# Triangular inverse of a decoder trunk: the eight transfers of inverted blocks into T issued from GpSimd, those into TT from SyncE

## The chip, the cores and the metric

The kernel runs on one core of a Trainium2 chip. A core has five engines with queues of their own: TensorE (PE in the profile, its weight loads PEld), VectorE (DVE), ScalarE (ACT), GpSimd (POOL) and SyncE (SP). An engine works through its queue in order; between engines only semaphores order the work. DMA transfers are issued from an engine's queue (here from SyncE, GpSimd and, a few, ScalarE) and run on the core's 16 DMA engines. The metric is device time in microseconds (us) of one execution.

## The reference, cut to what matters

A decoder trunk of two layers over 256 positions of width 1024. Each layer is a half-step gated feed-forward block, a mixer of two branches, and a second feed-forward block. The change lies in the mixer's gated delta-rule branch, which works in chunks of 64 positions for 8 heads:

```python
M = jnp.where(strict, jnp.einsum("bnhid,bnhjd->bnhij", kb, k) * decay, 0.0)
eye = jnp.eye(C, dtype=f32)
rhs = jnp.concatenate([v * beta[..., None], kb * jnp.exp(G)[..., None]], axis=-1)
sol = lax.linalg.triangular_solve(eye + M, rhs, left_side=True, lower=True, unit_diagonal=True)
```

The kernel does not solve; it inverts the unit lower triangular matrices `eye + M` (32 of 64 x 64, one for each head and chunk) and multiplies with the inverses.

## The kernel before, in words

**The stream of weights.** Nearly all of TensorE's work is products with weights that come once from HBM. SyncE loads them in blocks of 128 x 1024 (`wraw`, 512 KB, `load`, line 188) into five buffers in turn. ScalarE splits each block into a high part (`whi`, `prep`, through `act`, line 82), VectorE takes the rest (`wlo`, line 85), and TensorE multiplies with both (through `put`, line 60). A block's buffer comes free when VectorE is done with it, so SyncE's next load usually waits for VectorE.

**The order of the mixer.** The table `ORDER` (line 46) sets by hand in which order the pieces of the mixer are written: `k`, `q`, `v`, `z`, `b` and so on are products with weights, cut into steps; a capital `I` runs the generator `invert` on to its next `yield`. TensorE keeps that written order; the other engines' queues are set by a scheduler.

**The inverse** (`invert`, lines 925 to 986). The 32 matrices lie in pairs as 16 matrices of 128 x 128 in `Q`, each with 8 diagonal blocks of 16 x 16. The steps are:

1. Eight transfers bring the diagonal blocks of `Q` to DRAM (`dq1`), one transfer brings them back so that each partition holds one block (`X`).
2. VectorE inverts all 128 blocks at once in 15 steps (lines 941 to 945, tile `X2`) and writes the transposed copy beside them (line 946). The profile calls both `X`.
3. One transfer writes `X2` to DRAM (`dq2`, line 947; the profile says `dq`).
4. Sixteen transfers bring the inverted blocks back, one for each position on the diagonal: eight into `T` (line 950) and eight transposed into `TT` (line 951). Each moves 16 partitions x 16 matrices x 16 numbers, in runs of 64 bytes. `T` and `TT` were set to zero long before by GpSimd (line 789).
5. The blocks are joined to inverses of 32 and then of 64 (loop from line 961, `n` = 4 and 2): TensorE forms `yb` from `Q` and the odd column blocks of `TT`, ScalarE copies it out (`Y`), TensorE forms `wb` from `T` and `Y`, ScalarE copies that negated into `TT`, and for `n` = 4 VectorE turns 32 x 32 blocks of `TT` into `T` (line 985).

Between these products TensorE works at steps of `b3` (products `bc` in the profile), as `ORDER` has it: `b3:11 I b3:2 I b3:2 I b3`.

**Semaphores of transfers.** The scheduler gives SyncE's transfers eight completion semaphores in rotation, so a transfer waits until the eighth one ahead of it has landed. GpSimd's transfers have eight of their own. The first multiply of `yb` waits for four of the `TT` transfers (blocks 2, 4, 6 and 8); the first two multiplies of `wb` wait for four `T` transfers each, since one reads the left 64 columns of `T` and the other the right 64.

**GpSimd** does little: small powers for norms (line 227, `rsqrt`), products with them (line 889), zeroing (line 789), and transfers that add to their destination: weight blocks onto weight blocks (`wsum`, line 171) and partial sums onto `h` (line 494).

Of the kernel before, what the change touches and what calls it, by code (L numbers as in the profile page):

```python
# [51 lines left out]
def trunk_kernel(ctx, tc, x, wst, wsm, norms, lpar, rpar, cst, out):  # L52
    nc = tc.nc
    V, A, G = nc.vector, nc.scalar, nc.gpsimd
# [26 lines left out]
    def act(o, i, func=AF.Copy, **kw):  # L81
        return A.activation(out=o, in_=i, func=func, **kw)  # L82

    def tt(o, a, b, op):
        return V.tensor_tensor(out=o, in0=a, in1=b, op=op)  # L85
# [12 lines left out]
    def tmp2(name):  # L98
        return s2.tile([P, 512], F32, tag="s2", name=name)

    def trb(name):
        return trp.tile([P, 512], F32, tag="tr", name=name)
# [4 lines left out]
    def small(shape, name, bufs=2):  # L107
        return sm.tile(shape, F32, tag=name, name=name, bufs=bufs)
# [540 lines left out]
    def mixer(l, nxt):  # L649
# [135 lines left out]
        T = slots.tile([P, 16, P], F32, tag="sE", name="T")  # L785
# [139 lines left out]
        def invert():  # L925

            dq1 = dram.tile([P, 16, 16], F32, tag="dq1", name="dq1")
            dq2 = dram.tile([P, 2, 16, 16], F32, tag="dq2", name="dq2")
            for b in range(8):
                r0 = 16 * b  # L930
                nc.sync.dma_start(dq1[r0 : r0 + 16].rearrange("pr r s -> r pr s"), Q[r0 : r0 + 16, :, r0 : r0 + 16])
            X = s2.tile([P, 16, 16], F32, tag="s2", name="X")
            X2 = s2.tile([P, 2, 16, 16], F32, tag="s2", name="X2")
            with tc.issue_after(qev["ins"].ins):
                V.memset(X2[:], 0.0)
                V.memset(X2[:].rearrange("p a r s -> p (a r s)")[:, 0:256:17], 1.0)
            nc.sync.dma_start(X[:], dq1[:])
            yield
            Tl = X2[:, 0]
            tp = small([P, 64], "tp", 1)  # L940
            for c in range(15):
                n, m = 15 - c, c + 1
                t_ = tp[:, : n * m].rearrange("p (a b) -> p a b", a=n)
                tt(t_, X[:, c + 1 :, c : c + 1].to_broadcast([P, n, m]), Tl[:, c : c + 1, 0:m].to_broadcast([P, n, m]), ALU.mult)
                tt(Tl[:, c + 1 :, 0:m], Tl[:, c + 1 :, 0:m], t_, ALU.subtract)
            V.tensor_copy(X2[:, 1].rearrange("p r s -> p s r"), X2[:, 0])
            nc.sync.dma_start(dq2[:], X2[:])
            for b in range(8):
                r0 = 16 * b
                nc.sync.dma_start(T[r0 : r0 + 16, :, r0 : r0 + 16], dq2[r0 : r0 + 16, 0].rearrange("pr r s -> r pr s"))  # L950
                nc.sync.dma_start(TT[r0 : r0 + 16, :, r0 : r0 + 16], dq2[r0 : r0 + 16, 1].rearrange("pr r s -> r pr s"))
            yield

            def half_mm(bank, i, lhsT, rhs, w=64):
                for r in (0, 64):
                    PE.matmul(bank[r : r + 64, i * w : (i + 1) * w], lhsT[:, r : r + 64], rhs, start=True, stop=True)

            def odd(ap, n):
                return ap.rearrange("p (b o s) -> p b o s", b=n, o=2)[:, :, 1, :]

            for n in (4, 2):
                w = 64 // n
                order = (0, 1) if n == 4 else (1, 0)
                ys = [trb("yb") for _ in range(2)]
                ev = Y if n == 4 else [tmp2("Y2") for _ in range(2)]
                for half in order:
                    for i in range(8):
                        half_mm(ys[half], i, Q[:, 8 * half + i, :], odd(TT[:, 8 * half + i, :], n))
                    act(ev[half][:], ys[half][:])
                yield  # L970
                ws = [trb("wb") for _ in range(2)]
                for half in order:
                    for i in range(8):
                        half_mm(ws[half], i, T[:, 8 * half + i, :], ev[half][:, i * 64 : (i + 1) * 64])
                    pr = slice(8 * half, 8 * half + 8)
                    for b in range(n):
                        r0 = 2 * w * b
                        act(
                            TT[r0 : r0 + w, pr, r0 + w : r0 + 2 * w],
                            ws[half][r0 : r0 + w].rearrange("p (x b s) -> p x b s", x=8, b=n)[:, :, b, :],  # L980
                            scale=-1.0,
                        )
                        if n == 4 and b % 2 == 0:
                            blk = (slice(r0, r0 + 32), pr, slice(r0, r0 + 32))
                            V.transpose(out=T[blk], in_=TT[blk])
                yield
# [251 lines left out]
        def dn_branch(j):  # L1238
            yield from branch("d", 4, j)
            if j == 3:  # L1240
                m = tg[1]
                for t in range(2):
                    for n in range(2):
                        sl = slice(n * 512, (n + 1) * 512)
                        stt(m[:, t, sl], m[:, t, sl], 1.0, sums["d"][t][n][:], ALU.add, ALU.mult)

        sc, inv, rc = scalars(), invert(), recur()
        units = {"z": z_unit, "k": k_unit, "q": q_unit, "v": v_unit, "b": bcm, "d": zdm, "x": xs_unit, "g": gate, "N": dn_branch, "B": ss_branch}
        rests = {"K": k_rest, "Q": q_rest, "V": v_rest}
# [233 lines left out]
```

## Time and profile before

| | |
|---|---|
| time, median of 3 runs | 1536.88 us |
| lowest and highest | 1535.88 and 1537.06 us |
| the profiled execution's own time | 1536.77 us |
| its span, first to last instruction | 1534.5 us |
| busy share PE, DVE, ACT, POOL | 99%, 83%, 63%, 5% |
| granted TensorE clock | 0.999 |
| read from HBM | 291.43 MB, 191 GB/s over the span |
| share of the 16 DMA engines: q1 (SyncE), q0 (GpSimd) | 56.1%, 4.7% |

How to read it: the profile is one execution. A row of a timeline gives the start in us from the span's start, the duration, the engine, the line of the kernel, the operation, what it writes `<-` what it reads, and how many were merged (x). A bracket holds the idle time of the engine just before and what ended it. A letter q behind an engine's name (SPq, POOLq) means its queue, where transfers are issued: the duration of such a row is the issue, and the transfer itself ends later, at its landing. Lines of the helpers (60 for TensorE, 82 for ScalarE, 85 and 88 for VectorE) stand for many operations, so tiles tell them apart.

### The profile page before, as it was taken

The numbers are of one execution on the slowest core, as the hardware profiler recorded it, in microseconds if no ns is written. First come the engines' busy times: TensorE is split into PE (matmuls) and PEld (weight loads), VectorE is DVE, ScalarE is ACT, GpSimd is POOL, SyncE is SP. The second block draws the span as 40 slices with busy tenths as digits, with TensorE's granted clock in tenths as the row PEclk, the third lists the DMA queues.
The fourth block names the chain that finished last, engine by engine and source line by source line (L and its number), as shares of the span: only waits on it lengthen the run. The fifth ranks groups of instructions, "written<-read, shape, count | busy, mean of one in ns | idle before, by whom it ended". The sixth has DMA issues, their size and how long they took to land.

```text
span 1534.5 us, 29046 instructions
## 1 busy us (share of the span) xinstructions
PE 1515.0 (99%) x11460; PEld 1382.4 (90%) x11460; DVE 1270.7 (83%) x1939; ACT 962.2 (63%) x1560; POOL 79.8 (5%) x86
## 2 busy tenths in 40 slices
PE   8999999999999999999999999999999999999998
PEld 7999889989988888999999998899899888899997
DVE  6888978857999766888988889789579996688888
ACT  6656756865766645566665666587657765456655
POOL 0000010100000000000000002010000000000000
PEclk9999999999999999999999999999999999999999
DMA  7577666453656556667767767654455555556764
GB/s 286 183 227 237 194 214 209 143 151 126 206 167 204 166 178 208 190 197 241 222 207 223 227 196 229 207 183 138 154 183 160 189 188 169 182 173 205 232 219 138
DMA packets 95950, 297.33 MB, mean 194 GB/s; under 512 B 22517, under 2 KB 23493, under 8 KB 94790
## 3 DMA queue, kind: packets, MB, share of 16 engines
q1 hardware_dynamic: 91492, 282.56, 56.1%
q0 software_dynamic: 4032, 12.58, 4.7%
q8 instruction: 90, 1.47, 0.4%
q14 instruction: 46, 0.38, 0.1%
q10 hardware_dynamic: 290, 0.33, 0.1%
HBM read 291.43 MB, written 1.92 MB: 191 GB/s over the span
## 4 chain that ended last, share of the span: by engine, by line
PE 87%; DVE 6%; DMA 2%; ACT 2%; issue 2%; SPq 1%; POOL 0%; POOLq 0%; DVEq 0%; ACTq 0%
PE fc L60 29%; PE o L60 9%; PE t L60 9%; PE b L60 8%; PE p L60 7%; PE xs L60 4%; PE f L60 3%; PE kk L60 3%; PE bc L60 2%; PE zd L60 2%; PE qq L60 2%; DVE wlo L85 2%; DVE ca L88 2%; DMA wraw<-in_wst_dram 1%; PE ydb L60 1%
## 5 line engine op out<-in xcount | busy, mean ns | idle before, releaser
L85 DVE TENSOR_TENSOR wlo<-wraw,whi 128x1024 fp32r<-128x1024 f32 x464 | 559.7, 1221 | 110.1 <-ACT whi L82 105.0
L82 ACT ACTIVATE whi<-wraw 128x1024 fp32r<-128x1024 f32 x464 | 487.9, 1060 | 194.4 <-PE fc L60 43.8
L60 PE MATMUL fc<-uW,whi 128*128 128x256 f32 (+1 forms) x2600 | 444.1, 276 | 0.0
L60 PEld LDWEIGHTS fc<-uW,whi 128*128 128x128 f32 x2600 | 394.1, 188 | 3.1
L60 PE MATMUL fc<-uW,wlo 128*128 128x256 f32 x1280 | 356.2, 278 | 0.0
L60 PEld LDWEIGHTS fc<-uW,wlo 128*128 128x128 f32 x1280 | 240.6, 188 | 0.0
L60 PE MATMUL t<-whi,uW 128*128 128x512 f32 x512 | 168.0, 401 | 0.0
L82 ACT ACTIVATE whi<-wsum 128x1024 fp32r<-128x1024 f32 x80 | 85.0, 1063 | 79.0 <-PE fc L60 64.5
L85 DVE TENSOR_TENSOR wlo<-wsum,whi 128x1024 fp32r<-128x1024 f32 x80 | 97.6, 1224 | 30.9 <-ACT whi L82 27.9
L60 PEld LDWEIGHTS t<-whi,uW 128*128 128x128 f32 x512 | 95.5, 188 | 21.8 <-issue 2.4
L60 PE MATMUL t<-wlo,uW 128*128 128x512 f32 x256 | 100.4, 394 | 0.0
L60 PE MATMUL xs<-uW,whi 128*128 128x256 f32 x514 | 90.9, 280 | 0.0
L60 PEld LDWEIGHTS xs<-uW,whi 128*128 128x128 f32 x514 | 78.0, 188 | 0.3
L60 PE MATMUL b<-whi,bh 128*128 128x512 f32 x192 | 76.0, 396 | 0.0
L60 PE MATMUL b<-whi,bl 128*128 128x512 f32 x192 | 75.1, 391 | 0.0
L60 PE MATMUL b<-wlo,bh 128*128 128x512 f32 x192 | 74.8, 390 | 0.0
L60 PE MATMUL xs<-uW,wlo 128*128 128x256 f32 x256 | 71.0, 277 | 0.0
L60 PEld LDWEIGHTS t<-wlo,uW 128*128 128x128 f32 x256 | 48.1, 188 | 10.9 <-issue 1.0
L82 ACT ACTIVATE gh<-g 128x512 fp32r<-128x512 f32 x40 | 25.4, 634 | 44.1 <-DVE g L85 44.1
L82 ACT ACTIVATE whi<-wb 128x1024 fp32r<-128x1024 f32 x20 | 21.2, 1061 | 48.2 <-PE fc L60 45.3
L60 PE MATMUL p<-whi,bsa 128*128 128x512 f32 x144 | 49.0, 390 | 0.0
L60 PEld LDWEIGHTS xs<-uW,wlo 128*128 128x128 f32 x256 | 48.1, 188 | 0.0
(290 smaller groups left out, 3033.7 us busy)
## 6 DMA issues: line engine op xcount, KB each, us to landing
wraw<-in_wst_dram SPq DMA_DIRECT2D x464, 512.0 KB, 5.0
wsum<-in_wst_dram SPq DMA_DIRECT2D x20, 512.0 KB, 7.6
wb<-in_wst_dram SPq DMA_DIRECT2D x20, 512.0 KB, 6.2
wsum<-in_wst_dram POOLq DMA_DIRECT2D x20, 512.0 KB, 6.9
dc<-rdram SPq DMA_DIRECT2D x8, 1024.0 KB, 6.7
nw<-in_norms_dram SPq DMA_DIRECT2D x6, 512.0 KB, 6.3
h<-u POOLq DMA_DIRECT2D x8, 256.0 KB, 5.8
gb<-rdram SPq DMA_DIRECT2D x8, 256.0 KB, 4.2
```

The source lines that it names most:

```text
L60: return self.put(nc.tensor.matmul(*args, **kw))
L82: return A.activation(out=o, in_=i, func=func, **kw)
L85: return V.tensor_tensor(out=o, in0=a, in1=b, op=op)
L88: return V.scalar_tensor_tensor(out=o, in0=a, scalar=s, in1=b, op0=op0, op1=op1)
```

## The change

The eight transfers into `T` are issued from GpSimd (`G` is `nc.gpsimd`) and no longer from SyncE. Those into `TT` stay.

```diff
             nc.sync.dma_start(dq2[:], X2[:])
             for b in range(8):
                 r0 = 16 * b
-                nc.sync.dma_start(T[r0 : r0 + 16, :, r0 : r0 + 16], dq2[r0 : r0 + 16, 0].rearrange("pr r s -> r pr s"))
+                G.dma_start(T[r0 : r0 + 16, :, r0 : r0 + 16], dq2[r0 : r0 + 16, 0].rearrange("pr r s -> r pr s"))
                 nc.sync.dma_start(TT[r0 : r0 + 16, :, r0 : r0 + 16], dq2[r0 : r0 + 16, 1].rearrange("pr r s -> r pr s"))
             yield
```

The order of the rows on TensorE, VectorE and ScalarE stays the same. On SyncE's queue in the first layer's inverse, between the transfer that writes `dq2` and the weight blocks (`wraw`) that follow, the difference begins with these rows (a minus: only before; a plus: only after):

```order
 L947 DMA dq_3287<-X_3297 128x512
 L188 DMA wraw<-in_wst_dram 128x1024
-L950 DMA T<-dq_3287 16x16x16
-L951 DMA TT<-dq_3287 16x16x16
...
+L951 DMA TT<-dq_3287 16x16x16 x8
 L188 DMA wraw<-in_wst_dram 128x1024 x18
```

The two rows into `T` and `TT` stand there eight times in turn before; now eight rows into `TT` follow each other, and the weight blocks behind them stand eight rows further ahead. On GpSimd's queue at the same place, between the small products for the values (`c`) and the powers of the recurrence (`so`):

```order
 L227 TENSOR_TENSOR c_2314<-kq,mhalf 128x4
 L889 TENSOR_TENSOR c_2314<-c_2314,pq 128x4
+L950 DMA T<-dq_3287 16x16x16 x8
 L227 TENSOR_TENSOR so_2318<-so,mhalf 128x4 x4
 L227 TENSOR_TENSOR srr<-sss,mhalf 128x2 x4
```

Eight transfers are put in there, with no other row of GpSimd moved against another. The second layer has the same two places.

## The prediction

> **What bounds the kernel now.** I read the page first, then the waits and the timelines of each engine around the two places (one in each layer) where the inverted blocks travel. The page's busy times and the shares of the chain that ended last:
>
> ```profile
> PE 1515.0 (99%) x11460; PEld 1382.4 (90%) x11460; DVE 1270.7 (83%) x1939; ACT 962.2 (63%) x1560; POOL 79.8 (5%) x86
> PE 87%; DVE 6%; DMA 2%; ACT 2%; issue 2%; SPq 1%; POOL 0%; POOLq 0%; DVEq 0%; ACTq 0%
> ```
>
> TensorE's row is full, so a change gains only where PE stands still. It does so in the inverse. PE's timeline there, first layer and then second (start, duration, what ran, and in brackets the idle time ahead of it with what ended it):
>
> ```profile
> 322.56 2.08 PE L60 MATMUL yb<-TT,Q 128*64 128x64 f32 x64 [1.30 <-DMA TT<-dq]
> 326.40 2.26 PE L60 MATMUL wb<-Y,T 128*64 128x64 f32 x64 [0.86 <-ACT Y L82]
> 330.11 2.08 PE L60 MATMUL yb<-TT,Q 128*64 128x64 f32 x64 [0.55 <-ACT TT L82]
> ...
> 1079.49 2.08 PE L60 MATMUL yb<-TT,Q 128*64 128x64 f32 x64 [0.48 <-DMA TT<-dq]
> 1083.66 2.26 PE L60 MATMUL wb<-Y,T 128*64 128x64 f32 x64 [1.19 <-ACT Y L82]
> 1087.37 2.08 PE L60 MATMUL yb<-TT,Q 128*64 128x64 f32 x64 [0.56 <-ACT TT L82]
> ```
>
> The first product of the inverse (yb) waits for the last TT block to land; the second (wb) waits for ScalarE's copy Y of the first. That copy is late for another reason, which ScalarE's timeline shows, with the chain's row for the weight block it waits for:
>
> ```profile
> 324.80 1.06 ACT L82 ACTIVATE whi<-wraw 128x1024 fp32r<-128x1024 f32 x1 [4.96 <-DMA wraw<-in_wst_dram]
> 325.77 1.07 ACT L82 ACTIVATE Y<-yb 128x512 f32<-128x512 f32 x2
> ...
> 320.95 3.83 DMA wraw<-in_wst_dram
> ```
>
> ScalarE runs in order, and a weight split stands ahead of Y; the weight block behind that split was issued at 320.95 only. SyncE's queue shows why (its rows in the first layer, then in the second):
>
> ```profile
> 309.33 0.33 SPq L947 DMA_DIRECT2D dq<-X  x1
> 311.51 0.33 SPq L188 DMA_DIRECT2D wraw<-in_wst_dram  x1
> 311.94 0.38 SPq L950 DMA_DIRECT2D T<-dq  x1
> ...
> 315.77 1.16 SPq L951 DMA_DIRECT2D TT<-dq  x1
> ...
> 320.41 0.45 SPq L951 DMA_DIRECT2D TT<-dq  x1
> 320.95 22.07 SPq L188 DMA_DIRECT2D wraw<-in_wst_dram  x9
> ...
> 1066.71 0.33 SPq L947 DMA_DIRECT2D dq<-X  x1
> 1073.25 0.85 SPq L951 DMA_DIRECT2D TT<-dq  x1
> 1078.13 33.31 SPq L188 DMA_DIRECT2D wraw<-in_wst_dram  x12
> ```
>
> Between 311.94 and 320.95 SyncE issues nothing but the sixteen small transfers. So one queue makes both waits: the last TT goes out at 320.41, and the next weight block only after it.
>
> **What leaves SyncE.** Eight of the sixteen issues go; those that stay follow each other as they do now from 320.41 to 320.95 (0.54 with the next row, 0.49 within the series). One hitch stays: at 315.77 SyncE had waited for the weight block of 311.51, whose semaphore the eighth transfer behind it takes over:
>
> ```profile
> 311.51 4.25 DMA wraw<-in_wst_dram
> ```
>
> Before, that eighth transfer is the fourth TT; now it is the eighth TT. So seven TT go out from 311.94 on at 0.49 each, the last of the seven by 314.9; the eighth still starts at 315.77 and takes up to 1.16; the weight block follows at 316.97, not 320.95: 3.98 earlier. In the second layer, 1073.25 plus 0.85 gives 1074.14, not 1078.13: 3.99 earlier. How long these transfers take from issue to landing, and the one that writes dq2 ahead of them:
>
> ```profile
> L947 SPq DMA_DIRECT2D dq<-X x2: 326/326/326, 309.3 to 1066.7; - x2
> DMA to landing us min/median/max: 2.0/2.0/2.0
> ...
> L950 SPq DMA_DIRECT2D T<-dq x16: 377/447/457, 311.9 to 1077.1; - x16
> DMA to landing us min/median/max: 1.8/2.6/4.7
> ...
> L951 SPq DMA_DIRECT2D TT<-dq x16: 398/447/1156, 312.4 to 1077.6; - x16
> DMA to landing us min/median/max: 1.7/2.2/4.4
> ```
>
> The last TT lands at 315.77 + 2.2 to 4.4, so 318.0 to 320.2. PE reaches yb at 322.56 - 1.30 = 321.26, so the wait of 1.30 goes with 1.1 to spare; in the second layer 1073.25 + 4.4 = 1077.65 stands against 1079.49 - 0.48 = 1079.01, and 0.48 goes. The weight block lands at 316.97 + 3.83 = 320.8 and its split ends at 321.9, before the first half of yb is done (321.26 + 1.04 = 322.3): Y no longer stands behind it. So 0.86 goes, and 1.19 in the second layer in the same way. What is late next is the transposed copy into TT: it needs wb's result, as now, so the 0.55 and 0.56 stay. Sum, if T is there in time: 1.30 + 0.86 + 0.48 + 1.19 = 3.83 off.
>
> **What arrives on GpSimd.** POOL has nothing to do there; its next row is
>
> ```profile
> 345.91 1.01 POOL L227 TENSOR_TENSOR so<-so,mhalf 128x4 f32<-128x4 f32 x1 [63.01 <-DVE so L88]
> ```
>
> so nothing is queued behind the eight issues, and nobody waits for POOL until then. They can start when dq2 has landed, at 309.33 + 2.0 = 311.33 (1068.71 in the second layer). But no transfer of this shape has gone out from POOL before. Its issues so far, and the packets of its queue (q0):
>
> ```profile
> L171 POOL DMA_DIRECT2D wsum<-in_wst_dram x20: 862/868/1032, 53.3 to 1500.5; - x20
> DMA to landing us min/median/max: 5.6/6.9/8.8
> ...
> L494 POOL DMA_DIRECT2D h<-u x8: 864/864/880, 171.2 to 1510.9; - x8
> DMA to landing us min/median/max: 3.6/5.8/6.6
> ...
> q0 software_dynamic: 4032, 12.58, 4.7%
> ...
> h<-u POOLq DMA_DIRECT2D x8, 256.0 KB, 5.8
> ...
> DMA packets 4983, 2.34 MB, mean 138 GB/s; under 512 B 4416, under 2 KB 4416, under 8 KB 4981
> ```
>
> The 28 transfers of q0 make 4032 packets, 144 each (128 rows and 16 more). A T block is 16 rows of 16 runs of 64 B, 256 runs, so 272 packets; the last row above (the stretch from 309 to 326, with sixteen such transfers) bears that out: 4416 / 16 = 276. Price p of one issue on POOL: at least 0.87, if the issue is a fixed cost; at most 0.87 x 272 / 144 = 1.64, if every packet costs. SyncE's rows give the slope between: 128 rows cost 0.326 (dq2), 256 runs 0.447, a factor of 1.37. I take 0.87 x 1.37 = 1.19. [...]
>
> Price L from issue to landing: 1.8 to 4.7 for T on SyncE, 3.6 to 6.6 for h from POOL, which moves 256 KB and adds. I take 4.5, near the top of the first and below the middle of the second, since the weight blocks now start at 316.97 and the last T blocks run beside them. The eighth T lands 7p + L after the start: 8.33 + 4.5 = 12.8 by my values; bounds 7 x 0.87 + 1.8 = 7.9 and 7 x 1.64 + 6.6 = 18.1.
>
> Deadline: wb is reached at 326.40 - 0.86 = 325.54 now, and 1.30 earlier, 324.24, after; that is 12.91 after the start. In the second layer 1083.66 - 1.19 - 0.48 = 1081.99, 13.28 after the start. Its first multiply reads the left 64 columns of T and its second the right 64, so all eight blocks count. T arrives just in time by 0.1 and 0.5: the gain holds, but it hangs on p and L. Every microsecond beyond the deadline is lost one for one, since PE keeps its written order.
>
> **The rivals.** (1) T comes a little late: with p at 1.19 and L at 6.6 it lands at 14.9, late by 2.0 and 1.6. Then 3.83 - 3.6 = 0.2 off: 1536.5. For it: h's landings. Against it: T is sixteen times smaller. At p below 1.0 even L = 5.8 is in time. (2) T becomes the bound: p = 1.64 and L = 6.6, 18.1, late by 5.2 and 4.8; 10.0 - 3.83 = 6.2 slower: 1542.9. It turns slower than before at 15.07 (326.40 - 311.33) and 14.95. For it: if each packet costs; against it: wsum with 4 KB rows and h with 2 KB rows cost the same 0.87, so POOL's issue is not set by bytes, and on SyncE doubling the rows adds only 37%. (3) VectorE holds POOL up. The rows that bear on it:
>
> ```profile
> 274.52 1.22 DVE L85 TENSOR_TENSOR wlo<-wraw,whi 128x1024 fp32r<-128x1024 f32 x1
> ...
> 274.60 1.19 POOL L889 TENSOR_TENSOR c<-c,pq 128x4 f32<-128x4 f32 x1
> 282.70 0.20 POOL L889 TENSOR_TENSOR c<-c,pq 128x4 f32<-128x4 f32 x1
> ...
> 172.07 2.35 DVE L85 TENSOR_TENSOR wlo<-wraw,whi 128x1024 fp32r<-128x1024 f32 x2
> ...
> 172.45 0.87 POOL L494 DMA_DIRECT2D h<-u  x1 [0.32 <-DVE u L88]
> ```
>
> A POOL operation on data took 0.99 more beside a weight split on VectorE. If each issue lost that, p = 1.86 and T lands at 17.5: late by 4.6 and 4.2, 5.0 slower, 1541.8. Against it: the issue at 172.45 lay inside such a split and took its usual 0.87. [...] (4) The change does not reach the end: a later wait takes up the 3.83. Against it: PE is 99% busy and its other engines get ahead, not behind; then nothing changes, 1536.8.
>
> **How the numbers follow.** In time (7p + L up to 13.3 or so): 0.50. Late by some, rival 1: 0.25. Rival 2: 0.13. Rival 3: 0.05. Rival 4: 0.07. Against the profiled execution's own 1536.77 the likeliest case is 1532.9; against the median 1536.88, 1533.0. About 0.2%, 3.1 us, is what a measurement of this kernel can tell from no change; it lies at 1533.8, so the full gain passes it by 0.7 only, and a T block late by 0.4 in each layer puts it within. Faster 0.48, the same 0.36 (rivals 1 and 4 and the near misses), slower 0.16 (rivals 2 and 3 where they reach 1540). The range: below, all PE idleness of the two places gone (1.30 + 0.86 + 0.55 + 0.48 + 1.19 + 0.56 = 4.94) would be 1531.8, so 1531.9; above, rival 1 and the lighter half of rivals 2 and 3, up to 1539.9.
>
> **What would show it.** After: SyncE's weight block at about 317.0 and 1074.1; yb with no DMA wait; ScalarE's weight split no longer waiting near 5 us; wb starting near 324.2 and 1082.0; eight POOL issues from about 311.4 at about 1.2. Wrong: wb waiting for the DMA of T, POOL's issues over 1.4 apart or landings above 5; and if yb's wait stayed, the TT blocks would be held by something other than the queue.

## The result, and the profile after

| | before | after |
|---|---|---|
| time, median | 1536.05 us (15 runs, 1534.92 to 1537.70) | 1531.86 us (15 runs, 1530.69 to 1533.57) |
| ratio, 95% interval | | 0.9973 (0.9966 to 0.9981) |
| profiled span | 1534.5 us | 1531.1 us |
| granted TensorE clock | 0.999 | 0.999 |

The change makes the kernel 4.2 us faster (2.9 to 5.2). The page's busy times after:

```profile
PE 1514.8 (99%) x11460; PEld 1382.1 (90%) x11460; DVE 1270.7 (83%) x1939; ACT 962.8 (63%) x1560; POOL 88.1 (6%) x102
```

TensorE's work is the same (1515.0 before); what went is idle time. GpSimd has 16 instructions more and 8.3 us more to do. TensorE's timeline in the inverse, first layer and then second:

```profile
321.97 2.08 PE L60 MATMUL yb<-TT,Q 128*64 128x64 f32 x64
324.88 2.09 PE L60 MATMUL wb<-Y,T 128*64 128x64 f32 x64
328.43 2.08 PE L60 MATMUL yb<-TT,Q 128*64 128x64 f32 x64 [0.56 <-ACT TT L82]
...
1077.40 2.09 PE L60 MATMUL yb<-TT,Q 128*64 128x64 f32 x64
1080.32 2.08 PE L60 MATMUL wb<-Y,T 128*64 128x64 f32 x64
1083.86 2.08 PE L60 MATMUL yb<-TT,Q 128*64 128x64 f32 x64 [0.56 <-ACT TT L82]
```

Four brackets are gone (1.30, 0.86, 0.48, 1.19) and two stay (0.56 each, 0.55 and 0.56 before). Idle time in these six rows was 4.94 us and is 1.12: 3.82 off, inside the interval of the measured gain. SyncE's queue, with the weight block behind the eight transfers that are left:

```profile
310.12 0.33 SPq L947 DMA_DIRECT2D dq<-X  x1
...
312.72 4.55 SPq L951 DMA_DIRECT2D TT<-dq  x8
317.36 23.99 SPq L188 DMA_DIRECT2D wraw<-in_wst_dram  x9
...
1065.53 0.33 SPq L947 DMA_DIRECT2D dq<-X  x1
1068.13 5.08 SPq L951 DMA_DIRECT2D TT<-dq  x8
1073.31 34.87 SPq L188 DMA_DIRECT2D wraw<-in_wst_dram  x12
```

From `dq2`'s issue to the weight block it is 317.36 - 310.12 = 7.24 us, and was 320.95 - 309.33 = 11.62. (Such distances are compared, not starts: in the first layer `dq2` went out between 308.2 and 310.1 in the profiles of this study, though the change does not touch what stands ahead of it.) What that does on ScalarE:

```profile
321.65 1.06 ACT L82 ACTIVATE whi<-wraw 128x1024 fp32r<-128x1024 f32 x1 [1.03 <-DMA wraw<-in_wst_dram]
323.17 0.60 ACT L82 ACTIVATE Y<-yb 128x512 f32<-128x512 f32 x1 [0.47 <-PE yb L60]
```

The weight split waits 1.03 for its block, not 4.96, and Y now waits for TensorE, not for the split. And the transfers themselves, on GpSimd (issues in the first and second layer, then the durations of all sixteen and their landings, then the last one of the first layer alone) and on SyncE:

```profile
312.64 4.57 POOL L950 DMA_DIRECT2D T<-dq  x8 [28.93 <-DMA dq<-X]
1068.18 4.57 POOL L950 DMA_DIRECT2D T<-dq  x8 [29.12 <-DMA dq<-X]
...
L950 POOL DMA_DIRECT2D T<-dq x16: 562/569/668, 312.6 to 1072.2; - x16
DMA to landing us min/median/max: 3.9/4.9/5.5
...
L950 POOL DMA_DIRECT2D T<-dq x1: 562/562/562, 316.7 to 316.7; - x1
DMA to landing us min/median/max: 4.1/4.1/4.1
...
L951 SPq DMA_DIRECT2D TT<-dq x16: 302/447/1169, 312.7 to 1072.0; - x16
DMA to landing us min/median/max: 4.2/4.8/5.4
```

GpSimd takes 0.57 us an issue. The last T of the first layer goes out at 316.65 and lands 4.1 later, at 320.7; that of the second goes out at 1072.19 and lands 3.9 later, at 1076.1. Both are 4.2 us ahead of wb.

The queues' packets, SyncE's (q1) before, then SyncE's and GpSimd's (q0) after, hold something that the prediction did not expect:

```profile
q1 hardware_dynamic: 91492, 282.56, 56.1%
...
q1 hardware_dynamic: 87140, 282.30, 56.3%
q0 software_dynamic: 4544, 12.85, 4.9%
```

SyncE has 4352 packets fewer, 272 for each of the sixteen T transfers, as reckoned. GpSimd's queue had 4032 and has only 512 more, 32 for each. So the same block makes 272 packets when SyncE issues it and 32 when GpSimd does.

### The profile page after: what moved, and what is told of

It is laid out like the page before. It is cut to its first block, busy times and chain, and to the rows that moved or that the text cites. A ratio compares the mean times of both kernels' runs of the same rounds, so it can differ in the third digit from the quotient of the medians.

```text
span 1531.1 us, 29066 instructions
## 1 busy us (share of the span) xinstructions
PE 1514.8 (99%) x11460; PEld 1382.1 (90%) x11460; DVE 1270.7 (83%) x1939; ACT 962.8 (63%) x1560; POOL 88.1 (6%) x102
## 4 chain that ended last, share of the span: by engine, by line
PE 91%; DVE 4%; ACT 2%; DMA 2%; issue 1%; SPq 0%; POOL 0%; POOLq 0%; DVEq 0%; ACTq 0%
PE fc L60 29%; PE t L60 10%; PE o L60 9%; PE b L60 8%; PE p L60 7%; PE xs L60 6%; PE f L60 3%; PE bc L60 3%; PE zd L60 3%; PE kk L60 2%; PE qq L60 2%; DVE wlo L85 1%; PE ydb L60 1%; DVE ca L88 1%; PE vv L60 1%
## 5 line engine op out<-in xcount | busy, mean ns | idle before, releaser
L60 PEld LDWEIGHTS t<-wlo,uW 128*128 128x128 f32 x256 | 48.1, 188 | 11.2 <-issue 1.0
L171 POOL DMA_DIRECT2D wsum<-in_wst_dram x20 | 17.7, 886 | 576.1 <-DVE wlo L85 557.6
```

Source lines behind the costliest of these rows:

```text
L60: return self.put(nc.tensor.matmul(*args, **kw))
L171: G.dma_start(out=r[:], in_=tile_of(i), accum_op=ALU.add)
```

## The experiments

The theory to be tested is the prediction's: SyncE's queue alone makes both waits, by two paths. One is the last TT block (yb's wait); the other is the weight block behind all sixteen transfers, whose split on ScalarE stands ahead of Y (wb's wait). The rivals: that it is enough to bring TT earlier; that a second queue is what helps, whatever the order on the first; and, for what limits it, that T on GpSimd has no room. Each experiment is timed beside the kernel before.

**TT first, all sixteen on SyncE, every other engine's order as before.** The loop issues the eight TT and then the eight T, so the weight block still goes out behind sixteen. In `prep` and `invert` the copies of Y are told to come behind the weight split (`split`, the last but one written so far), which keeps ScalarE's rows as they stood:

```diff
-            for b in range(8):
-                r0 = 16 * b
-                nc.sync.dma_start(T[...], dq2[r0 : r0 + 16, 0]...)
-                nc.sync.dma_start(TT[...], dq2[r0 : r0 + 16, 1]...)
+            for b in range(16):
+                r0 = 16 * (b % 8)
+                d, o = (TT, 1) if b < 8 else (T, 0)
+                nc.sync.dma_start(d[...], dq2[r0 : r0 + 16, o]...)
...
-                    act(ev[half][:], ys[half][:])
+                    with tc.issue_after(split) if n == 4 else ExitStack():
+                        act(ev[half][:], ys[half][:])
```

> All sixteen transfers stay on SyncE, but the eight into TT go first and the eight into T after them; every other engine keeps the row order of before (ScalarE's weight split still ahead of Y). Theory A (the time hangs on when the next weight block is issued, since Y stands behind its split): the wait of yb for TT (1.30 and 0.48) goes, the weight block is still issued at about 321, and wb waits for Y by that much more, about 2.2 and 1.7; the time stays within 0.7 us of before. Rival B (the waits of yb and of wb are separate and add up; an earlier TT alone is worth its wait): 1.8 us faster.

Measured: 1536.71 us against 1536.67, ratio 1.0002 (0.9994 to 1.0011). TensorE's timeline in the first layer, of this kernel:

```profile
320.88 2.08 PE L60 MATMUL yb<-TT,Q 128*64 128x64 f32 x64
325.51 2.26 PE L60 MATMUL wb<-Y,T 128*64 128x64 f32 x64 [1.65 <-ACT Y L82]
```

yb's wait of 1.30 is gone, and wb's has grown from 0.86 to 1.65; in the second layer it is 1.76. On ScalarE the split still waits:

```profile
323.91 1.06 ACT L82 ACTIVATE whi<-wraw 128x1024 fp32r<-128x1024 f32 x1 [4.38 <-DMA wraw<-in_wst_dram]
324.87 1.07 ACT L82 ACTIVATE Y<-yb 128x512 f32<-128x512 f32 x2
```

So bringing TT earlier brings nothing: the weight block is the second end of the same wait. That rival's 1.8 us falls: the interval allows 0.9 us faster at most.

**TT first, with ScalarE's order left free.** The same loop without the added order. The scheduler then puts both Y ahead of the weight split, and the split between the copies into TT.

> As the run before, but ScalarE's order is left to the scheduler, which now puts both Y copies ahead of the weight split. SyncE is as busy as before and issues the weight block at about 321. Theory A, in its sharper form (the weight block matters only because Y stands behind its split): all four waits go, 3.3 to 4.2 us faster, the same as the change, without a second queue. Rival C (the product stream itself needs the weight block earlier, or the gain is that of a second queue): no more than 1.8 us faster, and a wait for weights shows on PE.

Measured: 1534.48 us, ratio 0.9989 (0.9981 to 0.9998), 1.7 us faster (0.3 to 2.9); less than expected, and by the time alone it could be rival C. But no wait for weights shows on TensorE. In its timeline the four waits are gone, but the one that stayed in the change has grown, here in the first layer (in the second it is 1.64 too):

```profile
328.90 2.09 PE L60 MATMUL yb<-TT,Q 128*64 128x64 f32 x64 [1.64 <-ACT TT L82]
```

ScalarE's timeline shows what is in the way:

```profile
325.48 1.13 ACT L82 ACTIVATE TT<-wb 16x128 f32<-16x128 f32 x4 [1.38 <-PE wb L60]
326.64 1.06 ACT L82 ACTIVATE whi<-wraw 128x1024 fp32r<-128x1024 f32 x1
327.72 1.13 ACT L82 ACTIVATE TT<-wb 16x128 f32<-16x128 f32 x4
```

A split of 1.06 stands in the middle of the copies into TT. 3.83 less 2 x 1.09 is 1.65, and 1.7 was measured: that row accounts for the miss, and the next experiment moves it.

**TT first, and the split between Y and the copies.** The same again, with the copies into TT told to come behind the weight split and given a higher priority:

```diff
-                        act(TT[...], ws[half]..., scale=-1.0)
+                        after = tc.issue_after(split) if n == 4 else ExitStack()
+                        with after, tc.high_priority(offset=PRI):
+                            act(TT[...], ws[half]..., scale=-1.0)
```

> All sixteen transfers on SyncE, TT first, as in tt_first, but ScalarE's order is set: both Y copies, then one weight split, then all eight copies into TT, then the next split. tt_first lost 1.09 per layer to a split among those eight copies. Theory A': what counts is which row ScalarE stands behind, not that SyncE is relieved: the four waits stay gone and yb's second wait is back at about 0.55 per layer, so 3.3 to 4.2 us faster than before, the whole gain of the change with one queue. Rival (a late weight block must be paid for somewhere, or a second queue is needed): 2.2 us or less, as tt_first.

Measured: 1533.36 us against 1537.48, ratio 0.9972 (0.9961 to 0.9983): as fast as the change, with one queue. TensorE waits for nothing but the copies (0.67 in the first layer, 0.61 in the second). On SyncE's queue the weight block is as late as before, 319.75 - 308.19 = 11.56 behind `dq2`:

```profile
308.19 0.33 SPq L947 DMA_DIRECT2D dq<-X  x1
...
310.79 4.93 SPq L951 DMA_DIRECT2D TT<-dq  x8
315.76 3.89 SPq L951 DMA_DIRECT2D T<-dq  x8
319.75 10.13 SPq L188 DMA_DIRECT2D wraw<-in_wst_dram  x7
```

ScalarE just doesn't wait for it ahead of Y any more:

```profile
322.81 0.60 ACT L82 ACTIVATE Y<-yb 128x512 f32<-128x512 f32 x1 [0.34 <-PE yb L60]
323.95 1.06 ACT L82 ACTIVATE whi<-wraw 128x1024 fp32r<-128x1024 f32 x1 [0.55 <-DMA wraw<-in_wst_dram]
```

So a second queue is not what helps. The wait is made where a late weight block meets ScalarE's fixed order, and either side can be moved: the block earlier (the change) or the split later (here).

**Two of eight, four of eight.** `(G if b < 2 else nc.sync).dma_start(T[...])`, then with `b < 4`; ScalarE's order held as in the first experiment.

> Only two of the eight T transfers go to GpSimd; all other orders as before. Theory A: the weight block comes 2 x 0.49 = 0.98 us earlier, wb's start follows it by 0.9 in each layer: about 1.8 us faster in all; wb still waits for Y, by about 1.2 and 0.8, and yb hardly waits. If the gain came from T's own queue or from fewer bytes on SyncE's ring rather than from the issue time: a quarter of the whole, 1.0 us, or nothing.

> Four of the eight T transfers go to GpSimd; all other orders as before. Theory A: the weight block comes 1.96 us earlier; wb waits for Y by 0.3 in the first layer and not in the second: 3.5 us faster, nearly all of the gain with half of the transfers, since beyond that PE is not ready sooner. Proportional to the number moved: 2.1 us.

Measured: 1534.95 us, ratio 0.9988 (0.9978 to 0.9997), 1.8 us faster (0.5 to 3.4); and 1534.02 us, ratio 0.9983 (0.9974 to 0.9991), 2.6 us faster (1.4 to 4.0). wb in the first layer, with two moved (in the second it waits 0.77, and yb still 0.33):

```profile
325.59 2.26 PE L60 MATMUL wb<-Y,T 128*64 128x64 f32 x64 [0.94 <-ACT Y L82]
```

and with four, where yb has no DMA wait in either layer, and wb none in the second:

```profile
323.25 2.26 PE L60 MATMUL wb<-Y,T 128*64 128x64 f32 x64 [0.16 <-ACT Y L82]
```

The times alone don't tell the theory from the rival: both intervals hold the theory's number (1.8 and 3.5) and the proportional one (1.0 and 2.1). The waits do. TensorE's idle time in the six rows is 4.94 us before, 3.13 with two moved, 1.25 with four and 1.12 with all eight. So with four of eight nearly all of the wait for Y is gone, and the last four have little left to remove.

**The other half.** TT from GpSimd, T on SyncE (`G` and `nc.sync` exchanged).

> The other half moves: the eight TT transfers go out from GpSimd, the eight T transfers stay on SyncE; all orders as in the changed kernel. GpSimd issues one each 0.57 us and its transfers land 4.9 after the issue, so the last TT lands 0.5 + 7 x 0.57 + 4.9 = 9.4 after dq2 has landed; PE reaches yb about 9.9 after. Theory A: just in time, 3.3 to 4.2 us faster, as the change; at worst a wait of up to 0.4 per layer in yb. Rival (it matters that the block needed first stays on the quick queue): yb waits 1 us or more in each layer, 2 us of the gain are lost.

Measured: 1532.92 us, ratio 0.9972 (0.9962 to 0.9982). TensorE waits 0.56 and 0.56 for the copies, as with the change, and GpSimd's issues cost the same (0.56 to 0.67 us, median 0.56).

Which half leaves SyncE makes no difference that these runs can tell.

**All sixteen from GpSimd**, TT first: the loop of the first experiment with `G.dma_start`. SyncE's weight block then goes out right behind `dq2`.

> All sixteen go out from GpSimd, TT first; SyncE has none, so the weight block goes out 8 us earlier than before. Theory A: earlier weights than in the changed kernel bring nothing, since PE no longer waits for them; T now lands 0.5 + 15 x 0.57 + 4.9 = 14.0 after dq2, PE reaches wb 12.9 after it: wb waits for T by about 1 us in each layer, and of the gain 1.5 to 2.2 us are left. Rival D (the less SyncE has to issue, the better): 4 us faster or more.

Measured: 1544.03 us against 1537.48, ratio 1.0042 (1.0028 to 1.0056): 6.5 us slower, wrong in size and sign. GpSimd's timeline:

```profile
311.15 4.57 POOL L951 DMA_DIRECT2D TT<-dq  x8 [28.73 <-DMA dq<-X]
315.80 0.56 POOL L951 DMA_DIRECT2D T<-dq  x1
318.75 3.89 POOL L951 DMA_DIRECT2D T<-dq  x7 [2.39 <-DMA TT<-dq]
```

Its tenth transfer waits 2.39 until one of the TT has landed (the program gives the completion semaphores of one engine's transfers out in turn, as SyncE's hitch at 315.77 showed before). The last T is issued at about 322.1, 11 us behind the first transfer, and TensorE stands:

```profile
325.98 0.30 PE L60 MATMUL wb<-Y,T 128*64 128x64 f32 x2 [1.64 <-DMA T<-dq]
327.63 3.49 PE L60 MATMUL wb<-Y,T 128*64 128x64 f32 x62 [1.35 <-DMA T<-dq]
```

In the second layer the two waits are 1.87 and 1.24. There is a second loss: wb itself takes 0.30 + 3.49, not 2.09. The stretches of one microsecond show why (the third number from the end is the granted clock; PE's busy time is the first behind the length):

```profile
327.00:328.00 1.00, 0.37 (x7) 0.40 (x9) 0.00 (x0) 0.00 (x0) 0.00 (x0) 0.70 0.73 131
...
330.00:331.00 1.00, 1.00 (x23) 0.99 (x20) 0.83 (x2) 0.71 (x3) 0.00 (x0) 0.59 0.00 0
```

Between them it is 0.50 throughout, so by the parts of these two rows the clock is halved at 327.4 and back at 330.8. The account: idle time in the rows of the two layers is 0.52 + 1.64 + 1.35 + 0.33 and 0.74 + 1.87 + 1.24 = 7.69, so 2.75 more than the 4.94 of before. From wb's start to the next yb, less waits, it is 4.69 and 5.47 us where the change has 2.99: 4.2 lost to the clock. Together 6.9, against 6.5 (4.3 to 8.6) measured.

**How much room T has.** The change, with memsets of 128x128 on GpSimd ahead of each T transfer, one and then four, into a tile that nobody reads:

```diff
+            pad, prev = small([P, 128], "pad", 1), None
...
+                for _ in range(1):
+                    with ExitStack() if prev is None else tc.issue_after(prev):
+                        prev = G.memset(pad[:], 0.0).ins
+                with tc.issue_after(prev):
-                G.dma_start(T[...], dq2[r0 : r0 + 16, 0]...)
+                    prev = G.dma_start(T[...], dq2[r0 : r0 + 16, 0]...).ins
```

> The change, with one small memset on GpSimd (128x128, on a tile that nobody reads) ahead of each of the eight T transfers; the order on every other engine stays, but for one pair of rows of the first feed-forward. A memset of that size is estimated at 0.2 us, from the rows of 128x2048 (1.81 us for sixteen times the elements) and 128x1 (0.1 us). It tells how much room T has. By the trace of the change the last T lands at about 321.5, wb comes at 324.88, so seven memsets (1.4 us) shift T without being felt: the ratio stays that of the change, 0.997, with no DMA wait on wb. If T had no room (the prediction's 'just in time by 0.1 and 0.5'), wb would wait about 1.3 and 0.9 us, 2.2 us in all: a ratio near 0.999.

> The same with four memsets ahead of each T transfer: 28 between the first and the last, about 5.6 us. The last T lands near 327.1 (second layer 1082.6), and wb, at 324.88 and 1080.32 without it, waits about 2.2 us in each layer: 4.4 us slower than the change, so level with the kernel before (ratio 1.000) if every microsecond beyond the deadline counts once. If TensorE's granted clock falls behind such a wait, as it did behind the waits of 1.64 + 1.35 and 1.87 + 1.24 us where all sixteen went out from GpSimd, another 1.5 to 2.5 us come in each layer in which it falls: a ratio up to 1.003. If T is not what wb waits for, nothing changes: 0.997.

Measured with one: 1532.63 us against 1536.86, ratio 0.9972 (0.9962 to 0.9981). The last T goes out at 317.55, 5.05 us behind the first (4.0 without the memsets), and in TensorE's timeline wb doesn't wait:

```profile
325.05 2.08 PE L60 MATMUL wb<-Y,T 128*64 128x64 f32 x64
```

T's landings lie 3.5 to 5.5 us behind their issues (median 4.5); even at 5.5 the last one would be there at 323.05, 2.0 ahead of wb. So T had room. With four: 1544.65 us, ratio 1.0050 (1.0036 to 1.0064), 7.8 us slower than before and so some 12 slower than the change: the direction is the expected one, the size is beyond the upper end. TensorE's timeline:

```profile
323.19 0.33 PE L60 MATMUL wb<-Y,T 128*64 128x64 f32 x2
327.89 3.65 PE L60 MATMUL wb<-Y,T 128*64 128x64 f32 x62 [4.37 <-DMA T<-dq]
...
1092.76 3.65 PE L60 MATMUL wb<-Y,T 128*64 128x64 f32 x62 [4.55 <-DMA T<-dq]
```

The waits are 4.37 and 4.55, not 2.2, for two reasons, which GpSimd's rows show: four memsets and an issue take 1.60 us (each memset 0.26, not 0.2), so the last T goes out 11.2 us behind the first, not 9.6; and it is in use 327.89 - 321.97 = 5.9 us later, not 4.9.

```profile
310.78 0.67 POOL L955 DMA_DIRECT2D T<-dq  x1 [28.48 <-DMA dq<-X]
311.44 1.02 POOL L953 MEMSET pad<- 128x128 f32 x4
...
321.97 0.56 POOL L955 DMA_DIRECT2D T<-dq  x1
```

And the clock falls in this wait, in both layers, to 0.50; its first and last stretch in the first layer:

```profile
325.00:326.00 1.00, 0.00 (x0) 0.00 (x0) 0.21 (x1) 0.00 (x0) 0.00 (x0) 0.95 1.07 325
...
332.00:333.00 1.00, 1.00 (x8) 0.87 (x8) 0.74 (x2) 0.68 (x3) 0.00 (x0) 0.64 0.00 0
```

From wb's start to the next yb, less the wait, it is 5.37 and 5.23 us, not 2.99: 4.6 by the clock, beside 8.92 - 4.94 = 3.98 more of waiting. 8.6 in all, against 7.8 (5.5 to 9.8) measured.

**The wait that stayed.** The change, with four of the eight negated copies into TT on VectorE, to see whether the 0.56 can be had as well:

```diff
-                        act(TT[...], ws[half]..., scale=-1.0)
+                        to, by = TT[...], ws[half]...
+                        if n == 4 and half == 0:
+                            ts(to, by, -1.0, ALU.mult)
+                        else:
+                            act(to, by, scale=-1.0)
```

> The changed kernel, and four of the eight negated copies of wb into TT (those of the first half) go to VectorE instead of ScalarE, so that the one wait that is left in the inverse (yb for TT, 0.56 per layer) may go. Theory A (that wait is the length of ScalarE's chain of eight copies, 2.29 us): it goes, and the time is up to 1.1 us under that of the changed kernel, about 4.9 us under before. Rival: VectorE does its weight split of 1.22 us first, so the copies come later than now and the wait stays or grows; no gain over the changed kernel.

Measured: 1533.25 us, ratio 0.9977 (0.9968 to 0.9986): no gain over the change that can be told. TensorE's wait is 0.34, not 0.56:

```profile
327.81 2.08 PE L60 MATMUL yb<-TT,Q 128*64 128x64 f32 x64 [0.34 <-ACT TT L82]
```

VectorE comes to its copies only behind a weight split of its own (1.23 us, from 325.29), so the two engines don't share the work from the start. At most 2 x 0.22 = 0.44 us was to be had, less than the runs tell apart.

No version here beats the change: it (0.9973), the other half (0.9972) and one queue with the new order (0.9972) stand level.

## Why the prediction was right, step by step

- **What bounds it**: right. The four waits that were to go went, the two that were to stay stayed, and the sum was 3.82 for 3.83. That they hang on SyncE's order, by TT and by the weight block that meets ScalarE's order, is shown by the first three experiments and by the waits in the dose.
- **The weight block**: right. 3.98 and 3.99 earlier were forecast; relative to `dq2` it is 4.38 and 3.64 (11.42 less 7.78 in the second layer, from 1065.53 to 1073.31).
- **The last TT**: right, at the upper end. It was to land 2.2 to 4.4 us behind its issue; in the second layer it is issued at 1072.04 and lands 4.2 later, at 1076.3, 1.1 ahead of yb (1077.40) where 1.4 were forecast. (For the first layer the trace gives no landing of it.) The 2.2 was not to be had, as the median of all is now 4.8; the last section comes back to that. TT, for which "1.1 to spare" was written, came nearer to its deadline than T did.
- **T "just in time by 0.1 and 0.5"**: the mis-sized step. The price p of an issue was taken at 1.19, between bounds of 0.87 and 1.64; it is 0.57, below the lower bound. Two premises were wrong. First, 272 packets were taken for a T block, which is SyncE's count; from GpSimd it makes 32, fewer than the 144 of the transfers that cost 0.87, so a price by packets would have come out below 0.87 and not above. Second, 0.87 was taken as the least that an issue can cost, though it came from transfers of 128 rows that add to their destination. Which of the differences (packets, rows, adding) makes those dearer stays open: no run here issues one shape both plain and adding. L was taken at 4.5; the median is 4.9, but the last T, which counts, takes 4.1 and 3.9. So the eighth T lands 8.1 and 7.9 us after the first issue, not 12.8, against a deadline of 12.2 and 12.1 (forecast 12.9 and 13.3): 4.2 us to spare. That is where luck came in: the gain was said to hang on p and L, and p was wrong by a factor of two in the direction that does no harm. One memset per transfer, 1.05 us in all, was not felt.
- **Rivals 1 and 2** (T late, T the bound) fell with p. But the way from lateness to time that they used, "every microsecond beyond the deadline is lost one for one", is too mild: T made late by 4.4 and 4.6 us cost some 12 us against the change, since the clock fell as well, to 0.50. Rival 2's 6.2 slower would have been about 10.8 by an estimate that adds the 4.6 that the clock cost there.
- **Rival 3** (VectorE holds GpSimd up): not seen. While GpSimd issues, from 312.64 to 317.22, VectorE is busy for 4.55 of the 4.58 us, and no issue took over 0.67, where the rival needed 1.86.
- **Rival 4** (taken up later): fell, since 4.2 (2.9 to 5.2) arrived of 3.82.
- **The time**: 1533.0 was forecast from a before of 1536.88; over fifteen runs before is 1536.05. The gain was forecast at 3.9 and measured at 4.2. For the same reason the median of 1531.86 lies 0.04 below the range's lower end, which stood for 5.0 us less than 1536.88.

## What to carry to other kernels

A wait that names a transfer can be that of a queue, and one queue can be late at two ends (here 1.30 us of yb's wait for TT and 0.86 of wb's for Y in the first layer): before gaining one, look up what is issued behind the last transfer, and which engine waits for that ahead of the work that matters (here ScalarE, 4.96 us ahead of Y). Bringing one of the two ends forward moved the wait to the other: the 1.30 went, and the 0.86 became 1.65. Move only as much as frees the queue: four of the sixteen transfers were nearly enough (1.25 us of waits were left, 1.12 with eight), and all sixteen made the second queue the bound (7.69). A price or a packet count that was read on one queue did not hold on another: 0.45 us and 272 packets on SyncE, 0.57 us and 32 packets on GpSimd.

## What the runs showed of the hardware

- A plain transfer of 256 runs of 64 B (16 KB) makes 32 packets and takes 0.56 to 0.67 us to issue on GpSimd; on SyncE it makes 272 and takes 0.45 (median). The adding transfers of 144 packets take 0.87 (median) on GpSimd. What the second issuing engine saved here was time of issuing, eight issues or about 4 us of SyncE per layer, and it took 3.8 us off TensorE's waits, since the weight split for which ScalarE had waited 4.96 us stood ahead of Y.
- In the kernel before, the small transfers landed later when they went out while the weight block issued ahead of them was under way (311.51 to 315.76, and 1068.89 to 1073.24). Of the TT transfers whose landing the trace gives, those issued within these stretches took 3.6 to 4.4 us, the one at 1073.25 took 2.5, and those behind it 1.7 to 2.0; 2.2 is the median of all. With all sixteen on SyncE, TT first and the new order on ScalarE, TT and T together took 1.8 to 4.7, median 2.4. In the change, with eight of GpSimd's beside them, TT took 4.2 to 5.4, median 4.8. How much of that is GpSimd's was not tried apart.
- The granted clock fell from 1.00 to 0.50 behind some short gaps of TensorE. With four memsets TensorE stopped at 323.5 and the clock fell at 325.9, 2.4 later. With TT first and the order held, it fell at 1086.8, 2.1 behind the start of the gap of 1.76 in the second layer, when wb had begun again at 1086.42:

```profile
1086.00:1087.00 1.00, 0.58 (x11) 0.58 (x13) 1.00 (x1) 1.00 (x3) 0.00 (x0) 0.90 0.99 233
```

  The gaps of 1.65 (the same kernel, first layer) and of 1.64 (the free order, both layers) had no such fall. Neither had one of 1.74 in the kernel before (6.00 to 7.74), nor the 2.61 us ahead of TensorE's first multiply in the change: in both profiles the clock is 1.00 in every microsecond up to 1527. So these runs give no threshold. That profiled execution with the fall at 1086.8, 1539.74 us, was the longest of its twelve (median 1536.71), so most of them may have had no such fall. The halved stretch is 3.4 us long there (1086.8 to 1090.2) and in the first layer with all sixteen on GpSimd (327.4 to 330.8); it is 6.8 us long in the second layer of that kernel (1088.6 to 1095.4) and in both layers with four memsets (325.9 to 332.7, 1090.5 to 1097.3).
